# Hybrid decoder layer: value-pass sums taken from PSUM by DVE, the norm factor moved behind the value passes, and the sliding-window keys used as filler

## The chip, the cores and the metric

The kernel runs on one NeuronCore of a Trainium2 chip, as a single launch. The metric is the device time of one execution in microseconds, the median of several. The core has five engines that run side by side: PE (TensorE, matrix products and transposes), DVE (VectorE), ACT (ScalarE), POOL (GpSimd) and SP, whose queue issues nearly all DMA here. PE reads SBUF and writes PSUM, which the kernel divides into banks of 128 x 512 fp32: four called `z`, two `m`, two `o`.

## The reference

One decoder layer on 512 tokens of width 2048, in fp32, cut to what matters:

```python
h = rmsnorm(x, ln_mix)
proj = h @ w_in                        # 2048 x 4608
sb_q, sb_k, sb_v, sw_q, sw_k, sw_v = split(proj)   # 1024 1024 1024 | 1024 256 256
sb_o = stick_breaking_attention(sb_q, sb_k, sb_v)  # 16 heads of 64, causal
sw_o = sliding_window_sink_attention(sw_q, sw_k, sw_v, sinks, slopes)
                                       # 16 query heads, 4 key/value heads, window 128
mixed = concat(rmsnorm(sb_o, sb_out_norm), rmsnorm(sw_o, swa_out_norm))
x = x + mixed @ w_out
h = rmsnorm(x, ln_ffn)
x = x + (silu(gate) * up) @ w_down     # gate, up = h @ w_gate_up; width 5632
return rmsnorm(x, ln_final)
```

## The kernel before

**Precision.** Each fp32 operand of a product is split into a high part (rounded, by ACT) and a low part (the difference, by DVE). A product is then three PE products: high by high, high by low, low by high. The splits of weights are called `whi` and `wlo` (`split`, lines 220 and 221), those of the normalized input `hhi` and `hlo` (`split_scaled`, lines 272 and 273). PE therefore computes only at the pace at which ACT and DVE split.

**The queue of slabs.** Most projections are a list `queue` of weight slabs of 512 KB, each with its groups of three products. `step()` emits one group; at the third group of a slab it loads the two slabs behind it and splits the next. `pull(ns)` emits groups worth `ns` of the planner's time (648 ns for a feature group), `drain(mark)` all up to a mark, `defer(n, fn)` calls `fn` after `n` groups. So slabs are *filler*: they are pulled between the steps of the attention loops. The framework may reorder instructions of an engine against program order by its own cost estimate, except those called through `pV`, `pA`, `pG`, `pT` and every `dma`, which keep their order on their engine.

**First phase, while x arrives.** `add_kq` (line 534) puts eight slabs of 256 rows into the queue. Each has 512 columns: the 256 sliding-window key columns and the first 256 query columns, loaded by two DMAs (slab 0 by four). `prep(s)` first calls `h_make(kt)` for the row tiles that the slab needs: PE transposes four 128 x 128 blocks of x into a PSUM bank, `split_scaled` makes `hhi` and `hlo` with the gain, and POOL adds the two into `hf`. The norm factor of a row is not needed for this; it is a scale on tokens, applied at evacuation. `x_squares` sums the squares. `rstd1_make` (line 343) makes the factor from them, on DVE and ACT, four groups after slab 5; `rstd1_rows` broadcasts it along rows, by four products of `ones` with a scaled identity `dg` (`row_bc`, line 290).

**Value passes.** The stick-breaking value projection is done in seven products instead of eight (a Strassen-like scheme, `ValuePass`, line 568) for each of two halves `g` of the rows: 28 slots, each with one product of 12 PE instructions. Its weight-side sums are POOL's (`sum`: differences of loaded blocks). Its activation-side sums are formed from `hf` by POOL as well, in blocks of 128 x 1024 (`diff`, `s1`, `s2`, `s4`), and each is split by ACT (`form(p, "h")`) and DVE (`form(p, "l")`) into a tile `vf`. What happens in which slot is written out by hand in a table (`at_slot`), with the stages load, sum, late and take. The stage load issues on SP. Behind the slots the value tiles are scaled with the norm factor and split into `vst` (`value_split`).

**Stick-breaking loop.** 64 jobs (16 heads by four blocks of keys), whose filler is the eight query/key units `add_qk` of four slabs and the sliding-window value slabs of `add_swv`, up to `sb_mark`; the last value slab stays for the next loop. Each job pulls a fixed amount:

```python
SBFILL = SB_SLABS * 8 * 648.0 / 62     # SB_SLABS = 30; SBFILL per step of 66
```

**Sliding-window loop.** 16 jobs (four groups of four query heads, four token blocks). Its keys must be stacked into `kst` and its queries into `qst` (high and low parts one over the other, `stack_two` and `stack_one`, lines 685 to 699, on ACT and DVE). Keys and query group 0 come from `kq`, the tile that the first phase filled; groups 1 to 3 are projected by `add_swq` as filler inside this loop, and the output projection's first half (`add_outA`, 16 slabs) is filler behind them. The loop is preceded by `pull(16000.0)` and pulls 5200 per step. `kq` and the sliding-window value tile `swv` share one buffer.

**Behind it** come the second half of the output projection, the gated feed-forward part, also in passes of seven products, and the last norm. The change does not touch them.

Of the kernel before, what the change touches and what calls it, by code (L numbers as in the profile page):

```python
# [37 lines left out]
def tile_hymba(ctx: ExitStack, tc: tile.TileContext, x, ln_mix, w_in, sb_norm, swa_norm,  # L38
# [236 lines left out]
    def rstd_from(ss, n, scale, name):  # L275
# [292 lines left out]
    class ValuePass(Block):  # L568
# [37 lines left out]
        def block(self, q):  # L606
            x = hf[2 * self.g + int(q[1]) - 1]
            return x[:, :, 0:256] if q[0] == "1" else x[:, :, 256:512]

        def diff(self):  # L610
            self.s3 = self.tile("t", [P, 4, 256], bufs=3)
            pG.tensor_tensor(out=self.s3, in0=self.block("11"), in1=self.block("21"), op=ALU.subtract)

        def s1(self):
            pG.tensor_tensor(out=self.block("21"), in0=self.block("21"), in1=self.block("22"), op=ALU.add)

        def s2(self):
            pG.tensor_tensor(out=self.block("11"), in0=self.block("21"), in1=self.block("11"), op=ALU.subtract)

        def s4(self):  # L620
            pG.tensor_tensor(out=self.block("12"), in0=self.block("12"), in1=self.block("11"), op=ALU.subtract)
# [10 lines left out]
    vp = [ValuePass(g) for g in range(2)]
    for g in range(2):
        b0, u = 14 * g, vp[g]
        for k, q, i in ((-6, "12", 0), (-6, "22", 0), (-5, "11", 0), (-4, "12", 1), (-3, "22", 1), (-2, "11", 1),
                        (0, "21", 0), (1, "21", 1)):
# [1 line left out]
        for k, p, i in ((-3, "7", 0), (-2, "5", 0), (-1, "7", 1), (0, "5", 1), (1, "6", 0), (2, "6", 1),
                        (3, "4", 0), (4, "4", 1)):
            at_slot(b0 + k, "sum", u.sum, p, i)  # L640
        for k, fn, *args in ((-5, u.diff), (-5, u.s1), (-4, u.s2), (-4, u.form, "7", "h"), (-3, u.form, "7", "l"),
                             (0, u.form, "6", "h"), (1, u.form, "6", "l"), (4, u.form, "5", "h"), (5, u.form, "5", "l"),
                             (5, u.s4), (7, u.form, "3", "h"), (8, u.form, "3", "l")):
            at_slot(b0 + k, "late", fn, *args)
# [1181 lines left out]
```

## Time and profile before

| | us |
|---|---|
| median of 3 runs | 2033.25 (2032.68 to 2034.13) |
| the profiled execution's own time | 2032.92 |
| its span, first to last instruction | 2031.2 |
| PE busy | 2004.4 (99%) |
| DVE busy | 1505.8 (74%) |
| ACT busy | 1502.5 (74%) |
| POOL busy | 1123.3 (55%) |

The span is that of the engines' instructions; the execution's own time holds 1.7 us around it. Busy time is summed over an engine's instructions. A row of a timeline gives start, duration, engine, line, operation, output and inputs, count, and in brackets the idle time of that engine just before, with the instruction that ended it. Helpers record their callers' operations on their own line (most pinned calls are on L118), so rows are told apart by tile names. The granted clock is 1.00 when PE runs at full speed, 0.50 at half.

### The profile page before, as it was taken

Reading aid. Unit: us, or ns where it says so; the run is one execution under the profiler, and the core shown is the slowest. Engines: PE = TensorE matmul, PEld = TensorE weight load, DVE = VectorE, ACT = ScalarE, POOL = GpSimd, SP = SyncE. Lnnn points to the kernel's source line nnn. Section 1 sums busy time; section 2 is a strip of 40 time slices with the busy share of each in tenths; the row PEclk is TensorE's granted clock in tenths of the full one; section 3 lists DMA queues with packets and bytes.
Section 4 is the critical chain, followed back from the end, with each engine's and each line's share of the span. In section 5 each row is a group of like instructions: output and inputs, shape, how many; then the busy total and the mean of one; then the engine's idle time right before and its main releaser. Section 6 shows DMA issues by size and latency. Waiting matters only on the chain.

```text
span 2031.2 us, 29381 instructions
## 1 busy us (share of the span) xinstructions
PE 2004.4 (99%) x10364; PEld 1705.1 (84%) x10364; DVE 1505.8 (74%) x2016; ACT 1502.5 (74%) x2061; POOL 1123.3 (55%) x605
## 2 busy tenths in 40 slices
PE   9999999989999999999999999999999999999998
PEld 8778888878888888888888888888888888888886
DVE  5786888876984777777777777777777867767767
ACT  6675877755872468777777777777777788778787
POOL 5851444430000047666676666766667678878883
PEclk9999999989999999999999999999999999999999
DMA  7122222112234354535445354453444743433423
GB/s 240 66 78 83 63 63 71 58 39 84 73 120 134 120 163 123 136 102 137 117 117 140 101 134 123 111 140 105 129 129 106 270 161 104 169 142 104 171 89 115
DMA packets 286515, 240.24 MB, mean 118 GB/s; under 512 B 11168, under 2 KB 237536, under 8 KB 283936
## 3 DMA queue, kind: packets, MB, share of 16 engines
q1 hardware_dynamic: 285696, 235.71, 39.0%
q8 instruction: 82, 1.34, 0.3%
q0 software_dynamic: 288, 1.32, 0.2%
q10 hardware_dynamic: 384, 1.34, 0.2%
q14 instruction: 65, 0.53, 0.1%
HBM read 218.40 MB, written 19.92 MB: 117 GB/s over the span
## 4 chain that ended last, share of the span: by engine, by line
PE 74%; DVE 2%; ACT 1%; DMA 1%; issue 0%; DVEq 0%; POOL 0%; ACTq 0%; POOLq 0%
PE o L118 34%; PE m L118 28%; PE m L364 1%; PE m L366 1%; PE m L365 1%; PE o L365 1%; PE o L366 1%; PE o L364 1%; PE z L118 1%; DMA raw<-in_w_out_dram 1%; PE m L398 1%; PE m L397 1%; PE m L396 1%; DVE wlo L221 0%; PE z L1092 0%; PE o L398 0%
## 5 line engine op out<-in xcount | busy, mean ns | idle before, releaser
L118 POOL TENSOR_TENSOR t<-raw,t 128x1024 f32<-128x1024 f32 x111 | 282.2, 2543 | 276.9 <-ACT hp L118 262.5
L118 DVE TENSOR_TENSOR wlo<-t,hp 128x1024 fp32r<-128x1024 f32 x247 | 300.9, 1218 | 180.2 <-PE o L118 108.5
L118 ACT ACTIVATE whi<-t 128x1024 fp32r<-128x1024 f32 x247 | 262.1, 1061 | 127.6 <-PE o L118 76.9
L118 POOL TENSOR_TENSOR t<-raw,raw 128x1024 f32<-128x1024 f32 x114 | 296.9, 2607 | 26.8 <-issue 11.7
L118 PE MATMUL o<-hca,whi 128*128 128x512 f32 x880 | 307.5, 391 | 0.0
L118 DVE TENSOR_TENSOR wlo<-raw,hp 128x1024 fp32r<-128x1024 f32 x187 | 228.1, 1220 | 86.0 <-issue 52.1
L118 ACT ACTIVATE whi<-raw 128x1024 fp32r<-128x1024 f32 (+1 forms) x189 | 199.6, 1056 | 104.1 <-PE m L118 74.5
L118 ACT ACTIVATE hp<-t 128x1024 fp32r<-128x1024 f32 x247 | 249.1, 1008 | 0.7 <-POOL t L118 0.7
L118 PE MATMUL o<-hca,wlo 128*128 128x256 f32 x880 | 244.0, 280 | 0.0
L118 ACT ACTIVATE hp<-raw 128x1024 fp32r<-128x1024 f32 x191 | 192.7, 1009 | 3.3 <-DMA raw<-in_w_down_dram 2.3
L118 PEld LDWEIGHTS o<-hca,whi 128*128 128x128 f32 x880 | 164.2, 187 | 35.8
L118 PE MATMUL m<-hca,whi 128*128 128x512 f32 x528 | 186.3, 392 | 1.1 <-DVE hca L118 1.1
L221 DVE TENSOR_TENSOR wlo<-raw,whi 128x1024 fp32r<-128x1024 f32 x87 | 109.6, 1260 | 88.1 <-ACT whi L220 87.5
L220 ACT ACTIVATE whi<-raw 128x1024 fp32r<-128x1024 f32 x87 | 91.7, 1054 | 102.8 <-PE o L366 40.2
L118 PEld LDWEIGHTS o<-hca,wlo 128*128 128x128 f32 x880 | 165.6, 189 | 0.4
L118 PE MATMUL m<-whi,dca 128*128 128x512 f32 x592 | 146.9, 389 | 0.0
L118 PE MATMUL o<-whi,dca 128*128 128x512 f32 x592 | 146.8, 389 | 0.0
L118 PE MATMUL m<-hca,wlo 128*128 128x256 f32 x528 | 146.3, 280 | 0.0
L118 PEld LDWEIGHTS o<-whi,dca 128*128 128x128 f32 x592 | 111.1, 188 | 23.0
L118 PEld LDWEIGHTS m<-whi,dca 128*128 128x128 f32 x592 | 111.0, 188 | 23.1
L396 PE MATMUL m<-hhi,whi 128*128 128x512 f32 x320 | 130.3, 407 | 0.0
L118 PE MATMUL m<-hcs,whi 128*128 128x512 f32 x352 | 125.9, 392 | 0.0
(384 smaller groups left out, 5304.2 us busy)
## 6 DMA issues: line engine op xcount, KB each, us to landing
raw<-in_w_gate_up_dram SPq DMA_DIRECT2D x348, 256.0 KB, 5.2
raw<-in_w_down_dram SPq DMA_DIRECT2D x68, 512.0 KB, 4.7
raw<-in_w_in_dram SPq DMA_DIRECT2D x78, 256.0 KB, 3.1
raw<-in_w_out_dram SPq DMA_DIRECT2D x32, 512.0 KB, 4.6
raw<-in_w_in_dram SPq DMA_DIRECT2D x28, 512.0 KB, 3.6
aT<-w SPq DMA_DIRECT2D x44, 256.0 KB, 3.4
xd<-aT SPq DMA_DIRECT2D x10, 1024.0 KB, 7.7
rx<-in_w_down_dram SPq DMA_DIRECT2D x20, 512.0 KB, 6.1
```

The lines of the kernel that those rows point to most:

```text
L118: return lambda *a, **k: tc.keep_in_program_order(fn(*a, **k))
L220: A.activation(out=hi, in_=raw, func=AF.Copy)
L221: V.tensor_tensor(out=lo, in0=raw, in1=f(hi), op=ALU.subtract)
L364: mm(o, lhsT=lh[:, sl], rhs=hi[:, j, :], start=first, stop=False, skip_group_check=halves)
L365: mm(o, lhsT=lh[:, sl], rhs=lo[:, j, :], start=False, stop=False, skip_group_check=halves)
L366: mm(o, lhsT=ll[:, sl], rhs=hi[:, j, :], start=False, stop=(k == nslab * a - 1), skip_group_check=halves)
L396: mm(o, lhsT=wh, rhs=xh, start=(k == 0), stop=False)
L397: mm(o, lhsT=wh, rhs=xl, start=False, stop=False)
L398: mm(o, lhsT=wl, rhs=xh, start=False, stop=(k == KT - 1))
```

## The change

1. **Sums from PSUM.** `hf` and POOL's four block sums go. `h_make` now hands the transposed bank to `left_sums(kt, pb)`. For the first four row tiles of a half, POOL adds 256 columns of high and low part, and DVE later subtracts that from the other 256 columns, read from PSUM and multiplied with the gain; for the next four tiles DVE does three such operations. They are kept in `vsum` and emitted behind the split of the row tile after. The four sums of a half live in two `v8` tiles (`vleft`).
2. **`form(p, "l")`** moves from DVE to POOL, and into the stage `sum`; loads and sums get other slots. The sum for product 4 is written over that for product 6.
3. **The norm factor** is made behind the last value slot, pinned in order on DVE and ACT (`pV`, `pA`); its broadcast goes by ACT and is deferred by ten groups.
4. **First phase: four query tiles** (512 adjacent columns, one DMA per slab, two for slab 0) instead of two key and two query tiles; two of the four evacuations by DVE.
5. **Keys as filler.** The key columns and query group 2 become eight slabs ahead of `add_swv`, evacuated into a new tile `kq2`. Query group 3 stays in the sliding-window loop. `pull(16000.0)` goes; the stacks of key pair 1 and query group 2 are made in steps 5 and 6 of the loop, in buffers that the input's splits have left.

```diff
@@ load
         if i == 0:
             for j in range(a):
-                for k, src in enumerate(srcs):
-                    dma(out=raw[:, j, k * n:(k + 1) * n], in_=src[j * P:(j + 1) * P, :])
+                dma(out=raw[:, j, :], in_=srcs[0][j * P:(j + 1) * P, :])
@@ h_make
-            hf.append(v8.tile([P, 4, 512], F32, tag="v8", name="hf"))
-        pG.tensor_tensor(out=hf[kt // 4][:, kt % 4, :], in0=f(h_hi[kt]), in1=f(h_lo[kt]), op=ALU.add)
+        if kt > 1:
+            while vsum:
+                vsum.pop(0)()
+        left_sums(kt, pb)
+
+    def left_sums(kt, pb):
+        g, j, gc = kt // 8, kt % 4, gcol[:, kt:kt + 1]
+        if kt % 8 == 0:
+            vs = [v8.tile([P, 4, 512], F32, tag="v8", name="vs") for _ in range(2)]
+            for k, p in enumerate("5736"):
+                vleft[g, p] = vs[k // 2][:, :, (k % 2) * 256:(k % 2) * 256 + 256]
+        s1, s3, s4, s2 = (vleft[g, p][:, j, :] for p in "5736")
+        a, b = pb[:, 0:256], pb[:, 256:512]
+
+        def stt(out, x, y, op):
+            V.scalar_tensor_tensor(out=out, in0=x, scalar=gc, in1=y, op0=ALU.mult, op1=op)
+
+        if kt % 8 < 4:
+            pG.tensor_tensor(out=s1, in0=f(h_hi[kt])[:, 256:512], in1=f(h_lo[kt])[:, 256:512], op=ALU.add)
+            vsum.append(lambda: stt(s3, a, s1, ALU.subtract))
+        else:
+            vsum.append(lambda: (stt(s1, b, s1, ALU.add), stt(s2, b, s3, ALU.subtract), stt(s4, a, s2, ALU.subtract)))
@@ rstd1_make, rstd1_rows
-        V.tensor_reduce(out=sst, in_=ss1, axis=AX.X, op=ALU.add)
-        rs1["c"] = rstd_from(sst, NT, 1.0 / D, "rstd1")
+        pV.tensor_reduce(out=sst, in_=ss1, axis=AX.X, op=ALU.add)
+        rs1["c"] = rstd_from(sst, NT, 1.0 / D, "rstd1", pV, pA)
...
-        rs1["b"] = row_bc(rs1["c"], "rbc1")
+        rs1["b"] = row_bc(rs1["c"], "rbc1", pz())
@@ add_kq
-                    A.activation(out=kq[0][:, c, :], in_=o, func=AF.Copy)
+                    if c % 2:
+                        A.activation(out=kq[0][:, c, :], in_=o, func=AF.Copy)
+                    else:
+                        V.tensor_copy(out=kq[0][:, c, :], in_=o)
...
-            queue.append(dict(srcs=[win[rows, C_SWK:C_SWK + 256], win[rows, C_SWQ:C_SWQ + 256]], a=2, b=512, big=None,
+            queue.append(dict(srcs=[win[rows, C_SWQ:C_SWQ + 512]], a=2, b=512, big=None,
@@ ValuePass.form and its table
-                pV.tensor_tensor(out=hl[:, :, 256:512], in0=src, in1=f(hl)[:, :, 0:256], op=ALU.subtract)
+                pG.tensor_tensor(out=hl[:, :, 256:512], in0=src, in1=f(hl)[:, :, 0:256], op=ALU.subtract)
...
-        for k, q, i in ((-6, "12", 0), (-6, "22", 0), (-5, "11", 0), (-4, "12", 1), (-3, "22", 1), (-2, "11", 1),
+        for k, q, i in ((-6, "22", 0), (-6, "12", 0), (-5, "11", 0), (-4, "11", 1), (-3, "12", 1), (-2, "22", 1),
                         (0, "21", 0), (1, "21", 1)):
...
+        for k, fn, *args in ((-4, u.sum, "7", 0), (-3, u.sum, "5", 0), (-2, u.form, "7", "l"), (-1, u.sum, "6", 0),
+                             (0, u.sum, "7", 1), (1, u.sum, "5", 1), (2, u.form, "6", "l"), (3, u.sum, "6", 1),
+                             (4, u.sum, "4", 0), (5, u.sum, "4", 1), (6, u.form, "5", "l"), (8, u.form, "3", "l")):
+            at_slot(b0 + k, "sum", fn, *args)
+        for k, p in ((-4, "7"), (0, "6"), (4, "5"), (7, "3")):
+            at_slot(b0 + k, "late", u.form, p, "h")
@@ behind the first phase, and behind the value slots
     drain_to(5, 3)
+    while vsum:
+        vsum.pop(0)()
     x_squares(4)
-    defer(4, rstd1_make)
...
     run(28, "take")
+    rstd1_make()
     open_z("psw")
...
-    defer(3, rstd1_rows)
-    defer(8, lambda: [value_split(1, t) for t in (3, 2, 1, 0)])
-    defer(14, kq_scale)
+    defer(10, rstd1_rows)
+    defer(12, lambda: [value_split(1, t) for t in (3, 2, 1, 0)])
+    defer(20, kq_scale)
...
+    kq2 = kqs.enter_context(tc.tile_pool(name="kq2", bufs=1, side="right", reuse_waits="tile")).tile([P, 4, 512], F32, name="kq2")
+    add_feat(win, [(C_SWK, 256)], two_m, lambda c, pb: k_evac(pb, kq2[:, c, :]))
+    add_feat(win, [(C_SWQ + 512, 256)], two_m, lambda c, pb: q_evac(pb, kq2[:, 2 + c, :]))
     add_swv()
@@ sliding window
-    for g in range(1, 4):
-        add_swq(g)
+    kst[0], qst[0], qst[1] = (v8.tile([P, 4, 512], F32R, tag="v8", name=n) for n in ("kst", "qst", "qst"))
+    stack_keys(0)
+    stack_queries(0, kq[0][:, 0:2, :])
...
+        def tiles():
+            kst[1], qst[2], qst[3] = act8("kst"), act8("qst"), act8("qst")
...
+    add_swq3()
+    swq3_end = len(queue)
...
-    pull(16000.0)
     at(swa_scores, 0)
+    stack_queries(1, kq[0][:, 2:4, :])
     for j in range(NJ + 2):
...
-        if j + 1 < NJ and jobs[j + 1][1] == 0:
-            drain(smarks[jobs[j + 1][0]])
+        if j == 5:
+            drain(swq3_end - 2)
+            stack_keys(1)
+        if j == 6:
+            stack_queries(2, kq2[:, 2:4, :])
+        if j == 10:
+            drain(swq3_end)
```

More of the change, by code (lines that the diff above doesn't have):

```diff
@@ L273, in split_scaled, with rstd_from @@
         V.scalar_tensor_tensor(out=lo, in0=ps_ap, scalar=g_ap, in1=f(hi), op0=ALU.mult, op1=ALU.subtract)
-    def rstd_from(ss, n, scale, name):
+    def rstd_from(ss, n, scale, name, V=V, A=A):
         v = sm.tile([P, n], F32, tag="rv", name="rv")
@@ L308, in tile_hymba @@
     h8 = [None, None]
-    h8s, hf = [], []
+    h8s, vsum, vleft = [], [], {}
     XC = [(0, 256), (256, 256), (512, 512), (1024, 512), (1536, 512)]
@@ L595, in sum @@
         def sum(self, p, i):
-            self.difference(p, i, self.raw["12", i] if p == "5" else self.tile("t", [P, 2, 512], bufs=3))
+            self.difference(p, i, self.raw["12", i] if p == "5" else self.t["6", i] if p == "4" else
+                            self.tile("t", [P, 2, 512], bufs=3))
         def left(self, p, k, half, c):
@@ L604, in left @@
             return vfm[self.g, p][:, k, c:c + P]
[L606 to L621, printed above, removed]
         def form(self, p, part):
-            src = self.s3 if p == "7" else self.block({"6": "11", "5": "21", "3": "12"}[p])
+            src = vleft[self.g, p]
             if part == "h":
@@ L634, in tile_hymba @@
         b0, u = 14 * g, vp[g]
-        for k, q, i in ((-6, "12", 0), (-6, "22", 0), (-5, "11", 0), (-4, "12", 1), (-3, "22", 1), (-2, "11", 1),
+        for k, q, i in ((-6, "22", 0), (-6, "12", 0), (-5, "11", 0), (-4, "11", 1), (-3, "12", 1), (-2, "22", 1),
                         (0, "21", 0), (1, "21", 1)):
             at_slot(b0 + k, "load", u.load, q, i)
[L638 to L644, printed above, removed]
+        for k, fn, *args in ((-4, u.sum, "7", 0), (-3, u.sum, "5", 0), (-2, u.form, "7", "l"), (-1, u.sum, "6", 0),
[4 more added lines that the diff above has]
+            at_slot(b0 + k, "late", u.form, p, "h")
         for k, p in enumerate(PD):
@@ L792, in kq_scale @@
         for c in range(4):
-            (k_evac if c < 2 else q_evac)(kq[0][:, c, :], kq[0][:, c, :])
-    defer(3, rstd1_rows)
-    defer(8, lambda: [value_split(1, t) for t in (3, 2, 1, 0)])
-    defer(14, kq_scale)
+            q_evac(kq[0][:, c, :], kq[0][:, c, :])
+    defer(10, rstd1_rows)
+    defer(12, lambda: [value_split(1, t) for t in (3, 2, 1, 0)])
+    defer(20, kq_scale)
     open_phase("sbp", 1)
@@ L973, in tile_hymba, with stack_keys, stack_queries, add_swq3 @@
     qst = [None] * 4
-    smarks = [0] * 4
-    def add_swq(g):
+    def stack_keys(c):
+        for e in range(2):
+            stack_two(kq2[:, c, :], e * HD, kst[c][:, 2 * e, :], kst[c][:, 2 * e + 1, :])
+    def stack_queries(g, src):
+        for c in range(2):
+            for e in range(2):
+                stack_one(src[:, c, :], e * HD, qst[g][:, c * 2 + e, :])
+    kst[0], qst[0], qst[1] = (v8.tile([P, 4, 512], F32R, tag="v8", name=n) for n in ("kst", "qst", "qst"))
+    stack_keys(0)
+    stack_queries(0, kq[0][:, 0:2, :])
+    def add_swq3():
         def done(c, pb):
-            if c == 0:
-                qst[g] = v8.tile([P, 4, 512], F32R, tag="v8", name="qst")
             qf = tmp(name="qf")
@@ L981, in done @@
             for e in range(2):
-                stack_one(qf, e * HD, qst[g][:, c * 2 + e, :])
-        add_feat(win, [(C_SWQ + g * 256, 256)], (lambda: [po(), po()]) if g == 1 else two_m, done)
-        smarks[g] = len(queue)
-    qst[0] = v8.tile([P, 4, 512], F32R, tag="v8", name="qst")
-    for c in range(2):
-        kst[c] = v8.tile([P, 4, 512], F32R, tag="v8", name="kst")
-        for e in range(2):
-            stack_two(kq[0][:, c, :], e * HD, kst[c][:, 2 * e, :], kst[c][:, 2 * e + 1, :])
-            stack_one(kq[0][:, 2 + c, :], e * HD, qst[0][:, c * 2 + e, :])
-    for g in range(1, 4):
-        add_swq(g)
+                stack_one(qf, e * HD, qst[3][:, c * 2 + e, :])
+        def tiles():
+            kst[1], qst[2], qst[3] = act8("kst"), act8("qst"), act8("qst")
+        n = len(queue)
+        add_feat(win, [(C_SWQ + 768, 256)], lambda: [po(), po()], done)
+        queue[n + 1]["post"] = tiles
+    add_swq3()
+    swq3_end = len(queue)
     mixA = [None] * 10
@@ L1134, in tile_hymba @@
         pull(SWFILL / 4)
+    kqs.close()
     drain()
```

1 line of the change is left out of this document (added).

## The prediction

> **What bounds the kernel now.** First I read the page: engines' busy shares and the TensorE clock.
>
> ```profile
> span 2031.2 us, 29381 instructions
> PE 2004.4 (99%) x10364; PEld 1705.1 (84%) x10364; DVE 1505.8 (74%) x2016; ACT 1502.5 (74%) x2061; POOL 1123.3 (55%) x605
> ...
> PEclk9999999989999999999999999999999999999999
> ```
>
> TensorE is the bound, and the change removes none of its products: the four query/key tiles of the first phase are 64 groups of three matmuls before and after, the other six tiles 96 groups, only in another order. So the time can move by PE's idle time, the clock lost behind it, and new waits, nothing else. Next, the busy time by stage, with my cuts at the places where PE is not full (columns: busy of PE, PEld, DVE, ACT, POOL, then clock, DMA share, GB/s):
>
> ```profile
> core 0: us, PE busy (x) PEld busy (x) DVE busy (x) ACT busy (x) POOL busy (x), PEclk, DMA share, GB/s
> 8.01:53.60 45.59, 45.49 (x226) 37.62 (x227) 27.11 (x34) 29.55 (x67) 27.56 (x22) 1.00 0.75 245
> 53.60:58.53 4.93, 0.39 (x3) 0.00 (x1) 4.93 (x4) 0.00 (x0) 4.85 (x3) 0.88 0.01 2
> 58.53:64.23 5.70, 5.70 (x14) 4.45 (x15) 4.38 (x2) 1.63 (x3) 5.62 (x3) 0.50 0.00 0
> 66.00:139.00 73.00, 72.87 (x321) 60.01 (x321) 56.31 (x59) 59.59 (x63) 52.50 (x21) 1.00 0.20 66
> 139.00:150.00 11.00, 8.90 (x41) 6.67 (x40) 10.22 (x16) 7.46 (x10) 1.07 (x4) 1.00 0.52 150
> 415.00:433.00 18.00, 14.26 (x78) 10.33 (x76) 16.33 (x31) 14.99 (x33) 8.75 (x15) 1.00 0.00 1
> 433.00:446.50 13.50, 10.60 (x39) 8.73 (x40) 9.70 (x22) 3.19 (x8) 2.47 (x4) 0.50 0.01 1
> 467.00:620.00 153.00, 151.76 (x767) 125.80 (x766) 132.59 (x324) 113.84 (x282) 8.81 (x7) 1.00 0.31 102
> ```
>
> Three seams lose time. **Seam 1**, 53.6 to 64.2: a stall of 4.54 us, and behind it 5.70 us at clock 0.50, of which half (2.85) is lost: 7.4. **Seam 2**, 139 to 150: 11.00 - 8.90 = 2.1. **Seam 3**, 415 to 446.5: 18.00 - 14.26 = 3.7 idle, then 13.50 - 10.60 = 2.9 idle and half of 10.60 (5.3) lost to the clock: 11.9. Together 21.4 us. The x phase (8 to 53.6), the value passes (66 to 139) and the sliding-window stage (467 to 620) are full. What makes each seam, from the timelines and the waits of PE:
>
> ```profile
> 53.60 0.39 PE L544 MATMUL m<-hlo,whi 128*128 128x512 f32 x1
> 58.53 0.79 PE L545 MATMUL m<-hhi,wlo 128*128 128x512 f32 x1 [4.54 <-DVE wlo L221]
> ...
> 48.08 1.04 ACT L220 ACTIVATE whi<-raw 128x1024 fp32r<-128x1024 f32 x1
> 48.21 1.83 DVE L283 TENSOR_TENSOR rt<-rr 128x4 f32<-128x4 f32 x1 [0.51 <-ACT rr L281]
> 50.27 2.26 DVE L285 TENSOR_SCALAR rt<-rt 128x4 f32<-128x4 f32 x1
> 52.76 4.58 DVE L298 TENSOR_SCALAR dg<-ident,rstd 128x128 f32<-128x128 f32 x2
> 57.26 1.21 DVE L221 TENSOR_TENSOR wlo<-raw,whi 128x1024 fp32r<-128x1024 f32 x1
> 148.23 0.47 DVE L298 TENSOR_SCALAR dg<-ident,rstd 128x128 f32<-128x128 f32 x2
> ...
> 50.10 4.86 POOL L118 TENSOR_TENSOR hf<-hf 128x1024 f32<-128x1024 f32 x2
> 57.33 3.36 POOL L118 TENSOR_TENSOR raw<-raw,rx 128x1024 f32<-128x1024 f32 x1
> ```
> ```profile
> PE o L118 <- ACT whi L118: 1.0, 1, 1.0
> PE z L299 <- DVE dg L298: 1.1, 1, 1.1
> ...
> PE z L1041 <- DVE qst L699: 1.8, 3, 0.9
> PE z L900 <- DVE e L862: 1.2, 1, 1.2
> PE m L364 <- DVE swv L273: 1.1, 1, 1.1
> ```
>
> Seam 1: the norm factor's small operations sit on DVE in front of the last weight split. Two 128x128 products that take 0.47 us together when POOL is idle took 4.58, and a 128x4 one 2.26, each ending as POOL's long sum ended. Seam 2: ACT's weight copy stood behind the first scaled value splits, and the factor's broadcast waited for DVE. Seam 3: the filler runs dry, and DVE has eight heads of key and query stacking to do among the last head's own steps.
>
> **The change part by part.**
>
> *Norm factor behind the value passes.* The chain leaves DVE's queue at 47 to 57 us. ACT's half of the last split ended at 49.1, so it can run about 50, ahead of PE's need at 53.6. Seam 1's 7.4 goes, if what takes DVE's place is cheap:
>
> ```profile
> L273 DVE SCALAR_TENSOR_TENSOR hlo<-z,gcol,hhi 128x512 fp32r<-128x512 f32 x16 | 11.2, 744 | 4.9 <-ACT hhi L272 4.9
> L298 DVE TENSOR_SCALAR dg<-ident,rstd 128x128 f32<-128x128 f32 x2 | 4.6, 2329 | 0.0
> ...
> L273 DVE SCALAR_TENSOR_TENSOR swv<-m,rstd,swv 128x256 fp32r<-128x256 f32 x3 | 1.4, 480 | 2.5 <-ACT swv L272 2.5
> ...
> L118 POOL TENSOR_TENSOR hf<-hhi,hlo 128x512 f32<-128x512 f32 x16 | 21.1, 1342 | 23.5 <-DVE hlo L273 23.5
> L118 POOL TENSOR_TENSOR t<-raw,raw 128x1024 f32<-128x1024 f32 x8 | 21.9, 2746 | 9.6 <-DMA raw<-in_w_in_dram 7.4 <-ACT whi L118 2.2
> ```
>
> *Sums by DVE from PSUM.* One sum for each of 8 row tiles and three for each of the other 8: 32 operations of 256 columns. The nearest row is the 256-wide one with a PSUM input, 0.48 us: 15.4 us more on DVE from 8 to 54. DVE had 27.1 busy there, 5.6 of it the norm chain: 27.1 - 5.6 + 15.4 = 36.9 of 45.6 us, 81%. Does that delay a split that PE needs? The tightest place is a block of two row tiles with three sums between them:
>
> ```profile
> 22.62 1.03 PE L118 MATMUL z<-ident,xt 128*128 128x128 f32 x8
> 28.95 1.47 PE L118 MATMUL z<-ident,xt 128*128 128x128 f32 x12
> ...
> 24.71 1.40 DVE L273 SCALAR_TENSOR_TENSOR hlo<-z,gcol,hhi 128x512 fp32r<-128x512 f32 x2
> ```
>
> Transposes at 22.6, splits at 24.7 to 26.1; with three sums between, the second ends at 27.5. Its products come one group of eight behind the slab's start (27.6), at about 30.3: 2.8 us of slack. The sums run one row tile late, so they do not wait for POOL's add, and the bank is reused four tiles on. Cost 0, covered by that slack. POOL does 8 adds of half the size (estimate from 1.34: 0.67 each, 5.4 us for 21.1) and loses the eight block sums; it gets eight low-part subtractions from DVE at 2.4 to 2.75. In the value passes it keeps its count, one operation per slot or less.
>
> *Loads.* Slabs with 512 adjacent columns save nine of SP's issues; PE is packed behind 8 us, so 0. The value passes' loads are reordered; the last lands in time:
>
> ```profile
> 47.31 0.88 SPq L100 DMA_DIRECT2D raw<-in_w_in_dram  x2
> ...
> DMA to landing us min/median/max: 4.5/5.2/6.1
> ...
> 460.14 1.23 DVE L221 TENSOR_TENSOR wlo<-raw,whi 128x1024 fp32r<-128x1024 f32 x1 [4.21 <-ACT whi L220]
> 465.58 1.23 DVE L221 TENSOR_TENSOR wlo<-raw,whi 128x1024 fp32r<-128x1024 f32 x1 [4.21 <-ACT whi L220]
> ```
>
> A filler slab is 5.44 us (460.14 to 465.58), a slot of the value passes half of it, 2.72. Last landing: 48.2 + 5.2 = 53.4. The passes now begin near 59; the sum on that load (product 3) is needed at 59 + 3 x 2.72 - 2.2 = 65 (two copies of 1.1 stand between). Four POOL operations of 2.4 to 2.75 from 53.4 on end by 64; the product that needs the fourth begins at 72.6, so it is needed at 70. Bounds of what the passes lose: 0 (they lose 0.13 now) to 8 (rival C); I take 0.5, since the margins are a few us.
>
> *Seam 2.* The value splits can no longer get ahead of the weight copy, and the broadcast, on ACT, is deferred by ten groups (6.8 us); its first reader comes after four slabs (21.8). Gain 2.1. New: the factor's chain, pinned behind the last take, could hold ACT's copy for the second slab; bounds 0 to 2, the size of the seam itself. I take 1.0.
>
> *Keys and queries as filler.* By the planner's costs the sticks' loop pulls 66/62 x 30 x 5.18 + 4.0 = 169.5, and has 28 slabs of 5.18 and three of 5.18 (value): 160.7. It runs dry 8.8 before its end, as seam 3 shows. Eight slabs more (43.5 us measured) leave some 33 behind the loop, in which the last head and the first stacks (half as many) hide. Seam 3's 11.9 goes. (The late value columns are still evacuated into the buffer that the stacked tiles hold, seam 3's wait of 1.1; it now comes free after four more stacks, some 2.8 us of DVE, while PE goes on in the other pair of banks: 0, and 1.1 if it does not.) Two of the first phase's four evacuations move to DVE, 0.7 each: the bank's next product comes two tiles later, 0. In exchange the sliding-window loop starts without the 16 us pull in front and has 21 slabs (114 us) for 18 steps. PE's own work there: 151.8 less about 20 slabs (109) is 43; so it has 43 + 114 = 157 us against a loop of about 150, near balance, with DVE at 132.59/153 = 87%. DVE's change inside: two evacuations and a group's stack fewer, one key stack more, about even. Bounds for the loop: -1.2 (today's idle) to +6 (half of seam 3 again); I take +2.0.
>
> **Sum**: 2032.9 (the profiled execution: 2031.2 of span, 1.7 around it; the median is 2033.25) - 7.4 + 0.5 - 2.1 + 1.0 - 11.9 + 2.0 = **2015.0**.
>
> **The rivals.**
>
> B. The attention seam moves instead of going: the first sliding-window jobs have no filler in front, the scores wait for the stacks, and half of 11.9 returns. For it: DVE is the engine PE waits for in that seam, and 87% leaves little. Against: 33 us of dense filler now stand between. 2015 + 6 = 2021.
>
> C. POOL and DVE shut each other out in the value passes. DVE has 28 splits of 1.22 (34.2 us), POOL 27 operations of 2.4 (64.8), of which some 14 us run before the first product; if two-input operations of the two exclude each other, 50.8 + 34.2 = 85.0 against 28 x 2.72 = 76.2: +9, so 2024. Against: from 66 to 139 POOL was busy 52.5 and DVE 56.3 of 73.0, with PE full. The Trainium skill, "SBUF — State Buffer", section "SBUF: two separate sides", states that rule: the shared port pair is an exclusive lock, taken also by a DVE operation with two SBUF inputs against a GpSimd one that reads SBUF. By it the change, which moves subtractions to POOL, would end at C's time. The trace bears out the stretched 128x128 products, not a full exclusion of two-input operations.
>
> D. Both come true, and the change does not do what it says: 2015 + 6 + 9 = 2030.
>
> E, slower. DVE becomes the bound while x arrives: the sums stand in order in front of the row tiles' low parts. Place: the seven slabs from 15 to 54 us. Each stall like seam 1's costs 7.4 with its clock, and the change gains 17.9: two such stalls leave it near today's time (2030), from the third on it is slower: 2037, and with four 2045. For it: 81% of an in-order queue. Against: 2.8 us of slack where three sums stand together, and it would take sums of over 1 us.
>
> **How the numbers follow.** The likeliest, all three seams closed, 0.60: 2015, by its bounds 2010.5 (no new loss at all, and 1.2 of the loop's idle gone) to 2020. B 0.15, C 0.11, D 0.08, E 0.06. A change of 0.2% (4 us) is about what a measurement of this kernel can tell from none. Faster is the first three, 0.86; same D, 0.08; slower E, 0.06. The range takes in B and C: 2010 to 2026, which leaves out 0.14 and the tails.
>
> **What would show it.** Right: PE without a gap from 8 to the passes' end near 136, clock 1.00 there; the passes' first product near 59; the factor's chain on DVE near 137 with operations of 0.2; no clock of 0.50 around the end of the sticks; stacks beside filler. Wrong: PE waits for a row tile's low part before 54 (E); waits for a weight copy behind a POOL sum in the passes (C); waits on scores, transposes or DVE's softmax steps at 440 to 590 (B), or filler exhausted before the loop's last job.

## The result, and the profile after

The changed kernel takes **2010.26 us** (median of 4 runs, 2009.47 to 2010.75) against 2033.02 (2032.68 to 2034.13, 4 runs): a ratio of 0.9887, 95% interval 0.987 to 0.9904, so some 23 us faster. The forecast was 2015.0, between 2010 and 2026, so the result lies 4.8 below the forecast and at the lower edge of the range: two of the four runs (2009.47 and 2009.9) are below it. The profiled execution of after took 2010.75, with a span of 2009.0. All times and ranges here are of fast runs; one run of the filler experiment (2465 us, granted clock 0.752) and two of before measured beside the experiments (3873 and 6546 us) were slow ones and are not counted.

The page of after, the lines that answer to those of before:

```profile
span 2009.0 us, 29374 instructions
...
PE 1992.6 (99%) x10364; PEld 1700.1 (85%) x10364; DVE 1498.7 (75%) x2038; ACT 1503.0 (75%) x2063; POOL 1106.1 (55%) x597
...
PEclk9999999999999999999999999999999999999999
```

PE does the same 10364 products. The 8 in the clock's row is gone. The busy time by stage, cut at the same places of the program (columns as before):

```profile
7.69:51.50 43.81, 43.07 (x216) 35.66 (x217) 35.48 (x60) 29.38 (x65) 14.21 (x14) 1.00 0.71 239
51.50:56.40 4.90, 4.90 (x23) 4.06 (x22) 1.15 (x2) 0.00 (x0) 4.90 (x3) 1.00 0.65 241
...
59.13:135.29 76.16, 76.16 (x337) 63.08 (x336) 49.79 (x54) 60.74 (x63) 51.98 (x22) 1.00 0.22 70
135.29:146.00 10.71, 10.71 (x51) 8.60 (x50) 8.57 (x17) 7.53 (x16) 1.07 (x4) 1.00 0.35 101
...
415.00:434.00 19.00, 18.26 (x85) 14.59 (x85) 17.65 (x29) 14.07 (x24) 5.86 (x8) 1.00 0.18 56
434.00:447.00 13.00, 13.00 (x81) 11.71 (x81) 6.25 (x7) 2.65 (x3) 1.29 (x1) 1.00 0.41 122
447.00:460.00 13.00, 13.00 (x111) 13.00 (x110) 2.86 (x4) 2.12 (x2) 0.34 (x1) 1.00 0.26 82
460.00:510.00 50.00, 49.96 (x282) 43.15 (x282) 46.82 (x124) 40.38 (x104) 0.81 (x2) 1.00 0.26 85
510.00:532.00 22.00, 19.17 (x95) 15.30 (x95) 20.65 (x55) 18.20 (x44) 2.26 (x1) 0.92 0.31 96
```

The three seams are closed: PE is full, at clock 1.00, where 51.50, 135.29 and 434.00 begin. One new hole stands at 510 to 532, at clock 0.92, with DVE busy 20.65 of 22.00. The longest waits of PE in the whole trace show it too:

```profile
PE m L384 <- DVE wlo L220: 1.9, 1, 1.9
PE o L118 <- POOL ones L127: 1.2, 1, 1.2
PE m L118 <- DVE hca L118: 1.1, 1, 1.1
PE m L564 <- DVE wlo L220: 0.7, 1, 0.7
```

The 0.7 is a new wait for a weight's low part at 15.5 us; the 1.2 stands at the very start, ahead of PE's first instruction, and the 1.1 in a later stage (at 733 us). Both were there before, and the change leaves them alone.

Where the time came from is read by the lead of after at the same instruction, the start in before less that in after:

| the first | before | after | lead |
|---|---|---|---|
| product | 8.01 | 7.69 | 0.32 |
| value product | 66.28 | 59.13 | 7.15 |
| stick query/key product | 144.22 | 135.29 | 8.93 |
| stick score | 173.18 | 163.22 | 9.96 |
| product of the output's second half | 643.54 | 621.30 | 22.24 |

The lead stays at 9.95 through the sticks' loop, to about 390. So the first phase gave 7.1 (0.3 of it ahead of the first product, so 6.8 for seam 1, net of the new wait of 0.7), the value passes with seam 2 gave 2.8, seam 3 with the sliding-window loop 12.3.

For seam 3 and the loop I count PE's loss from the starts of its products: the time from one start to the next, less the median of that distance for the shape, summed in bins of 10 us. This sees the half clock and idle time alike, and holds within about 0.5 us. The seam, 410 to 450, lost 16.9 in before and loses 1.2 in after; the sliding-window loop, from 500 on, lost 3.7 and loses 5.5. By the lead the loop lost 3.4 more than before, as the remainder (-15.7 + 3.4 = -12.3); what the count from 500 on does not hold of it lies in bits below 1 us from 460 on.

### The profile page after: what moved, and what is told of

Same layout as the page of the kernel before. It is cut to its first block, busy times and chain, and to the rows that moved or that the text cites. A ratio compares the mean times of both kernels' runs of the same rounds, so it can differ in the third digit from the quotient of the medians.

```text
span 2009.0 us, 29374 instructions
## 1 busy us (share of the span) xinstructions
PE 1992.6 (99%) x10364; PEld 1700.1 (85%) x10364; DVE 1498.7 (75%) x2038; ACT 1503.0 (75%) x2063; POOL 1106.1 (55%) x597
## 4 chain that ended last, share of the span: by engine, by line
PE 96%; DVE 2%; ACT 1%; issue 0%; DMA 0%; SPq 0%; POOL 0%; DVEq 0%; ACTq 0%
PE o L118 36%; PE m L118 30%; PE m L415 4%; PE m L416 4%; PE m L417 4%; PE m L384 2%; PE m L385 2%; PE m L383 2%; PE z L118 1%; PE o L385 1%; PE o L384 1%; PE o L383 1%; PE o L935 1%; PE z L851 1%; PE z L850 1%; PE z L914 0%
## 5 line engine op out<-in xcount | busy, mean ns | idle before, releaser
L118 DVE TENSOR_TENSOR wlo<-t,hp 128x1024 fp32r<-128x1024 f32 x247 | 301.1, 1219 | 184.3 <-PE o L118 113.0
L118 POOL TENSOR_TENSOR t<-raw,t 128x1024 f32<-128x1024 f32 x111 | 281.9, 2539 | 281.9 <-ACT hp L118 269.5
L118 ACT ACTIVATE whi<-t 128x1024 fp32r<-128x1024 f32 x247 | 262.0, 1061 | 125.8 <-PE o L118 76.0
L118 PE MATMUL o<-hca,whi 128*128 128x512 f32 x880 | 307.5, 391 | 0.0
L118 POOL TENSOR_TENSOR t<-raw,raw 128x1024 f32<-128x1024 f32 x114 | 294.5, 2586 | 21.3 <-issue 10.8
L118 DVE TENSOR_TENSOR wlo<-raw,hp 128x1024 fp32r<-128x1024 f32 x187 | 228.3, 1221 | 92.2 <-issue 52.1
L118 ACT ACTIVATE whi<-raw 128x1024 fp32r<-128x1024 f32 (+1 forms) x189 | 199.8, 1057 | 105.4 <-PE m L118 75.2
L118 ACT ACTIVATE hp<-t 128x1024 fp32r<-128x1024 f32 x247 | 249.1, 1009 | 2.5 <-POOL t L118 2.5
L118 PE MATMUL o<-hca,wlo 128*128 128x256 f32 x880 | 244.0, 280 | 0.0
L118 ACT ACTIVATE hp<-raw 128x1024 fp32r<-128x1024 f32 x191 | 192.8, 1009 | 3.8 <-DVE wlo L118 2.2
L118 PEld LDWEIGHTS o<-hca,whi 128*128 128x128 f32 x880 | 164.2, 187 | 35.8
L118 PE MATMUL m<-hca,whi 128*128 128x512 f32 x528 | 186.3, 392 | 1.1 <-DVE hca L118 1.1
L118 PEld LDWEIGHTS o<-hca,wlo 128*128 128x128 f32 x880 | 165.6, 189 | 0.4
L118 PE MATMUL m<-whi,dca 128*128 128x512 f32 x592 | 146.9, 389 | 0.0
L118 PE MATMUL o<-whi,dca 128*128 128x512 f32 x592 | 146.9, 389 | 0.0
L118 PE MATMUL m<-hca,wlo 128*128 128x256 f32 x528 | 146.3, 280 | 0.0
L118 PEld LDWEIGHTS m<-whi,dca 128*128 128x128 f32 x592 | 111.1, 188 | 23.0
L118 PEld LDWEIGHTS o<-whi,dca 128*128 128x128 f32 x592 | 111.1, 188 | 23.1
L118 PE MATMUL m<-hcs,whi 128*128 128x512 f32 x352 | 125.9, 392 | 0.0
```

Source lines behind the costliest of these rows:

```text
L118: return lambda *a, **k: tc.keep_in_program_order(fn(*a, **k))
```

## The experiments

**The three parts by themselves.** First the norm factor, put back into DVE's queue four groups after slab 5 in the kernel after:

```
     x_squares(4)
+    defer(4, rstd1_make)
...
     run(28, "take")
-    rstd1_make()
```

> The changed kernel with the norm factor made where it was before, on DVE four groups behind slab 5, and its broadcast by DVE; all else as changed. Theory (each seam has its own cause, and the factor's small operations on DVE are that of the first two): the stall at about 51 to 56 us comes back with its half clock, and the value splits get ahead of the weight copies again: 7 to 10 us on 2010.3, so 2017 to 2020. Rival (the sums taken from PSUM freed POOL, and without POOL's long sums the chain on DVE is cheap): 2010 to 2013.

Measured: 2017.39 us (2016.15 to 2018.43), 7.1 more than after, in the theory's range. Its timeline, rows of DVE and POOL alone:

```profile
50.57 1.22 DVE L220 TENSOR_TENSOR wlo<-raw,whi 128x1024 fp32r<-128x1024 f32 x1
51.93 2.40 POOL L118 TENSOR_TENSOR vf<-vs,vf 128x1024 fp32r<-128x1024 f32 x1 [2.32 <-ACT vf L118]
51.98 2.37 DVE L282 TENSOR_TENSOR rt<-rr 128x4 f32<-128x4 f32 x1 [0.19 <-ACT rr L280]
54.28 4.75 POOL L118 TENSOR_TENSOR t<-raw,raw 128x1024 f32<-128x1024 f32 x2
54.38 2.31 DVE L283 TENSOR_TENSOR rt<-rt,rv 128x4 f32<-128x4 f32 x1
56.72 2.34 DVE L284 TENSOR_SCALAR rt<-rt 128x4 f32<-128x4 f32 x1
...
59.29 2.46 DVE L297 TENSOR_SCALAR dg<-ident,rstd 128x128 f32<-128x128 f32 x2
61.68 0.68 DVE L571 COPY kq<-m 128x512 f32<-128x512 f32 x1
```

The last weight split is now ahead of the chain and on time, so the stall stands elsewhere than forecast: four operations of the chain end with a POOL sum (those that meet none keep 0.16), and the `kq` evacuation behind them frees PE's bank 3.0 us late (`L118 <- DVE kq`), with the half clock after it. By the starts of the same products, this run is behind after by 3.4 at the first value product, 6.2 at the first stick query/key product and 7.2 at the first stick score, so the 7.1 holds seam 2 as well as seam 1. The price is that of the chain beside POOL's sums, wherever PE meets DVE's queue next.

Then the factor's place alone, in the kernel before (the same lines, the other way round):

> The kernel before with one part of the change: the norm factor made behind the value passes, pinned, its broadcast by ACT and deferred by ten groups. Theory: seams 1 and 2 go, seam 3 stays: 2033.0 - 7.4 - 2.8 = 2022.8, between 2021.5 and 2024.5. Rival (POOL's sums are what delays DVE there): half of it or less, 2028 to 2033.

Measured: 2025.57 (2025.2 to 2027.47), 7.7 less than before (2033.28 on that chip), short of the 10.2 forecast and outside its range of 2021.5 to 2024.5. Seams 1 and 2 are gone, and a wait that neither kernel has stands in the value passes (PE's longest wait of the first 160 us, then rows of the timeline):

```profile
PE m L118 <- ACT whi L118: 1.9, 1, 1.9
```
```profile
50.54 1.06 ACT L118 ACTIVATE vf<-t 128x1024 fp32r<-128x1024 f32 x1 [1.10 <-POOL t L118]
50.58 6.61 POOL L118 TENSOR_TENSOR hf<-hf 128x1024 f32<-128x1024 f32 x2
...
57.15 2.40 POOL L118 TENSOR_TENSOR t<-raw,raw 128x1024 f32<-128x1024 f32 x1
...
70.14 1.03 ACT L118 ACTIVATE hp<-t 128x1024 fp32r<-128x1024 f32 x1 [3.69 <-POOL t L118]
```

With the seam closed, the passes begin 7 us earlier, and POOL, which works without a break from 48.1 to 72.4 with two block sums (6.61) in that stretch, makes its weight sums late. The passes take 78.6 from their first product to the next stage's, 76.2 in after; these 2.4 are nearly all that the gain fell short by (2.5), and show what taking the sums off POOL is good for beside the first part. The whole change leads before by 9.96 at the first stick score, this part alone by 7.4.

The sums by DVE from PSUM alone, in the kernel before (`left_sums`, the low parts on POOL, the new table of slots; the factor early):

> The kernel before with one part of the change: activation sums by DVE from PSUM, low parts of the forms by POOL, the new slots of loads and sums; norm factor early, key tiles first. Theory: the first stall stays, since the factor's chain is still in DVE's queue beside POOL's weight sums: 2031 to 2035. Rival (less POOL work lets the chain through): 2024 to 2028.

Measured: 2030.06 (2028.7 to 2031.94), ratio 0.9986 (0.9976 to 0.9996), 3.2 less. That lies between the theory (2031 to 2035) and the rival (2024 to 2028), so neither forecast holds. The chain is again drawn out (2.37, 2.31, 2.34 and 2.51), but the last weight split stands ahead of it, as in the first run: seam 1's wait of 4.5 is gone, and PE waits 1.4 (at 16.5 us) and 1.6 (at 63.7) for low parts of weights and 0.8 and 1.1 in seam 2.

Queries first and keys as filler alone, in the kernel before:

> The kernel before with one part of the change: four query tiles in the first phase, keys and query group 2 as eight slabs of filler ahead of the value slabs, no pull in front of the sliding-window loop. Theory: seams 1 and 2 stay, seam 3 goes and the loop loses some 5 us: 2033.0 - 12.3 = 2020.7, between 2019 and 2023. Rival (the seam only moves into the loop): 2026 to 2033.

Measured: 2019.79 (2019.12 to 2019.83), ratio 0.9932 (0.9913 to 0.9952), 13.5 less: as expected. Seam 1's wait of 4.6 stays; PE's busy time in 400 to 450 is 49.26 of 50.00; and the loop has the hole of after already:

```profile
PE m L544 <- DVE wlo L220: 4.6, 1, 4.6
PE m L364 <- DVE wlo L220: 1.9, 1, 1.9
```

Together -7.7 - 3.2 - 13.5 = -24.4, against -22.8 for the whole: the parts overlap by under 2 us. The overlap lies ahead of the sticks: at the first stick score the three lead before by 7.4, 4.9 and 1.2, 13.5 in sum, and the whole change by 9.96, for the factor and the sums both relieve seam 1. From there on the third part gives 12.2 alone and 12.3 in the whole.

**What closed seam 3: more filler, or fewer stacks?** Two runs in the kernel before, with less filler asked for in each step of the sticks' loop, meant to leave some for its end and behind it:

```
-SB_SLABS = 30
+SB_SLABS = 28      (the second run: 24)
```

> The kernel before, with the sticks' loop planned for 28 slabs of filler in place of 30, so that by the planner's costs it pulls 158.6 of the 160.7 us that it has and does not run dry. Before is 2033.3. Theory 'filler' (seam 3 is PE without filler, all of it): the loop keeps its filler to the end and the seam's 16.8 us, as counted from the starts of PE's products, go: 2015 to 2020. Theory 'both' (1.84 + 3.69 = 5.5 us between 410 and 430 are the missing filler, the 11.2 us between 430 and 450 are DVE's eight heads of key and query stacking, which PE waits for with no filler behind the loop): 2026 to 2030, with the wait for qst and the half clock near 433 to 446 still there. Theory 'stacks alone': 2032 to 2034.

> The kernel before, with the sticks' loop planned for 24 slabs of filler in place of 30 (28 changed nothing): the loop takes some 26 of its 31 slabs, and what is left, about 25 us, is drained between the loop and the sliding-window scores, with the eight heads of stacking on DVE as before. Before is 2033.2. Theory 'filler behind the loop' (seam 3's 16.8 us are the tail of the last head and the stacks with no product of PE's beside them, so filler there closes it, whatever the number of stacks): 2017 to 2023, with PE over 95% from 420 to 450; the swv wait of 1.1 may stay. Rival 'half the stacks' (eight heads on DVE are too long for the seam even beside filler, and the change closed it by having four): 2026 to 2032, waits for qst still there. A third: a loop with a sixth less filler waits for its own DVE and ACT chains, and gives back what the seam gains: 2028 to 2036, with the lost time before 410.

Measured: 2035.48 with 28 (2034.87 to 2036.59) and 2037.68 with 24 (2036.48 to 2038.65); before is 2033.2. Both are slower than before and outside every range forecast for them. With 28, the seam (400 to 450) loses 16.9, as before. With 24, it still loses 15.5, and the sticks' loop (200 to 410) 10.4 in place of 2.7. Stages of the second run, PE's waits from 400 on, and its last filler product ahead of the scores with the next one:

```profile
430.00:440.00 10.00, 7.43 (x35) 5.21 (x34) 9.69 (x17) 8.25 (x15) 3.94 (x5) 0.81 0.01 2
440.00:450.00 10.00, 7.64 (x25) 5.48 (x26) 6.65 (x16) 2.28 (x6) 1.79 (x2) 0.50 0.01 2
```
```profile
PE z L903 <- DVE l L868: 2.5, 3, 1.0
PE z L1041 <- DVE qst L699: 1.5, 3, 0.8
```
```profile
434.47 0.28 PE L366 MATMUL m<-whi,hlo 128*128 128x256 f32 x1
435.19 0.39 PE L1041 MATMUL z<-kst,qst 128*128 128x256 f32 x1 [0.44 <-DVE qst L699]
...
449.82 0.58 PE L364 MATMUL m<-whi,hhi 128*128 128x256 f32 x1
```

The edit did not do what it was meant to. For 15.3 us, in which the last head's products wait for their low parts (`l`) and the scores for the stacks, PE has no filler product; in before it is 15.7. The reason stands in the program: `sb_begin` drains the queue up to a head pair's own query/key slabs before that pair starts, so what a step does not pull is pulled there in a lump. By the planner's costs these drains take 7.8 us with 30 slabs, 16.8 with 28 and 34.4 with 24, and the queue is empty at the 60th or 61st of the 66 steps in all three. So neither run had filler behind the loop, and neither tests the theory "filler behind the loop" or its rival "half the stacks". The time lost before 410, which the third theory forecast, is seen; the lumps are the likely cause, but that is not shown.

The reverse, in the kernel after: the stacks as there, and the filler used up.

```
-SB_SLABS = 30
+SB_SLABS = 37.5
```

> The kernel after, with the sticks' loop planned for 37.5 slabs of filler in place of 30: by the planner's costs it asks for 210.9 of the 202.1 us that it has, and so runs dry 8.8 before its end, as the kernel before does; the four heads of stacking at the seam stay as in after. After is 2010.3, and its seam loses 1.2 us of PE where that of before loses 16.8. Theory 'both needed' (24 slabs in the kernel before showed that filler does not close the seam beside eight heads of stacks; here four heads without filler): half of the loss returns, 8 us, and the wait with the half clock: 2016 to 2021. Rival 'half the stacks is all': the seam stays closed or loses 1 to 4: 2008 to 2014. A third, 'filler is all': the whole seam returns, 14 to 17 us: 2023 to 2028.

Measured: 2019.97 (2019.55 to 2020.78), 9.7 more than after, in the range of "both needed". The seam, now at 450 to 480 since the loop holds more filler, loses 10.3 in place of 1.2:

```profile
460.00:480.00 20.00, 13.83 (x77) 12.15 (x77) 17.66 (x44) 9.98 (x28) 2.86 (x4) 0.83 0.11 28
```
```profile
468.73 0.69 DVE L704 TENSOR_TENSOR qst<-kq,qst 64x512 fp32r<-64x512 f32 x1
...
469.45 0.84 ACT L271 ACTIVATE swv<-m,rstd 128x256 fp32r<-128x256 f32 x2 [2.39 <-DVE qst L704]
...
470.18 1.05 ACT L219 ACTIVATE whi<-raw 128x1024 fp32r<-128x1024 f32 x1
...
471.29 0.79 PE L415 MATMUL o<-hhi,whi 128*128 128x512 f32 x1 [4.76 <-ACT whi L219]
```

Its form is worth a look: PE waits 4.76 for a weight copy, which stands on ACT behind the evacuation of `swv`, which waited for the last query stack (the two share a buffer). So that buffer, priced at 0 to 1.1 in the prediction, takes part in a wait of this size once no filler covers it.

Here the edit did what it says, and it isolates the filler: the stacks are those of after. Over the runs, the seam's loss goes with the time that PE is without a filler product:

| run | no filler product on PE | loss of the seam | operations for stacks on DVE there |
|---|---|---|---|
| before | 15.7 (427.5 to 443.3) | 16.9 | 16 |
| before, 28 slabs | 15.4 (430.6 to 446.0) | 16.9 | 16 |
| before, 24 slabs | 15.3 (434.5 to 449.8) | 15.5 | 16 |
| after, filler used up | 9.4 (461.9 to 471.3) | 10.3 | 14 |
| after | 2.0 (458.4 to 460.4) | 1.2 | 14 |

The stacks differ less than "eight heads against four": 16 operations of DVE in before (11.0 us), 14 in after (8.7), of which 10 stand ahead of the first scores in the program. In after the last one ends at 436.2, 23 us before the first score:

```profile
435.55 0.69 DVE L704 TENSOR_TENSOR qst<-kq,qst 64x512 fp32r<-64x512 f32 x1
```
```profile
459.38 0.36 PE L1061 MATMUL z<-kst,qst 128*128 128x256 f32 x1
```

So filler is needed: shown. Whether fewer stacks are needed as well is open: no run has the stacks of before beside filler, and the 23 us of room speak against it.

**The new hole in the loop.** DVE's part of it in after, a query stack in the middle of the steps and the weight split that PE waits for:

```profile
515.26 0.69 DVE L704 TENSOR_TENSOR qst<-kq,qst 64x512 fp32r<-64x512 f32 x1
...
516.85 2.09 DVE L704 TENSOR_TENSOR qst<-kq,qst 64x512 fp32r<-64x512 f32 x3
...
525.84 1.22 DVE L220 TENSOR_TENSOR wlo<-raw,whi 128x1024 fp32r<-128x1024 f32 x1
...
527.12 0.65 PE L384 MATMUL m<-wlo,mhi 128*128 128x512 f32 x1 [1.85 <-DVE wlo L220]
```

Four ways to relieve it, each an edit of after. The two stacks spread over four steps:

```
-        if j == 5:
+        if j == 4:
             drain(swq3_end - 2)
-            stack_keys(1)
-        if j == 6:
-            stack_queries(2, kq2[:, 2:4, :])
+        if j in (4, 5):
+            stack_keys(1, (j - 4,))
+        if j in (6, 7):
+            stack_queries(2, kq2[:, 2:4, :], (j - 6,))
```

> The kernel after, with the second key stack and the third query stack of the sliding-window loop, which stand in steps 5 and 6, spread over steps 4 to 7, half a stack in each (drain of their filler one step earlier). After is 2010.3. Theory 'burst' (the wait of 1.9 us for a weight split at 527 and the half clock behind it come from these two stacks in DVE's queue, 98% full from 510 to 532): about 4 of the loop's 5 us of loss go, 2005.5 to 2008.5, no clock of 0.50 near 530. Rival 'balance' (DVE is simply full in this stretch, and what is moved shows up a step later): 2009.5 to 2011.5, with a wait of the same size elsewhere between 500 and 540. A third: draining a step earlier takes filler from the steps ahead: 2011.5 to 2014.

The same stacks' DVE part on POOL (`stack_keys(1, G)`, `stack_queries(2, ..., G)`):

> The kernel after, with the subtractions and copies of the same two stacks (second keys, third queries, steps 5 and 6) on POOL, which is nearly idle there, and ACT's part as it is. After is 2010.3. Theory 'DVE's queue': 12 operations of 0.4 to 0.7 us, some 7 us, leave DVE between 500 and 527, the weight split is on time: 2005.5 to 2008.5, no clock of 0.50 near 530. Rival 'ACT or balance': the split's other half by ACT is late as well, or the stretch is full otherwise: 2009.5 to 2011.5. A third: POOL's operations take twice as long and shut out DVE's two-input ones, so the scores that need the stacks wait: 2011 to 2014.

More filler for each step (`SWFILL = 5900.0` for 5200.0):

> The kernel after, with 5.9 planner-us of filler for each step of the sliding-window loop in place of 5.2 (18 steps: 12.6 us more, out of the some 17 us that PE still does from this queue behind the last step). After is 2010.3. Theory 'balance' (from 500 to 532 DVE is full; more PE work for each step gives DVE time, so PE waits less): of the loop's 7 to 8 us of loss 2 to 4 go, 2006.5 to 2008.5. Rival 'chain' (the waits are of the steps' own softmax chain and the order of DVE's queue, and more filler also brings more weight splits to DVE): 2009.5 to 2011.5. A third: the queue is empty before the last step, and the end of the loop has a seam of its own: 2011.5 to 2015.

Half the maxima:

```
-        for b in range(2):
-            V.tensor_reduce(out=mx[:, 2 * b:2 * b + 2], in_=B.s[b][:, :, 0:kw], axis=AX.X, op=ALU.max)
+        V.tensor_reduce(out=mx[:, 0:2], in_=B.s[0][:, :, 0:kw], axis=AX.X, op=ALU.max)
+        V.tensor_copy(out=mx[:, 2:4], in_=mx[:, 0:2])
```

> The kernel after, with the row maximum of the sliding-window scores taken over the first pair of heads alone and copied for the second (left out: 16 of 32 reductions, 15 us of them 0.68 each with the copy at 0.16, so DVE is relieved of some 8 us in the loop, 0.5 in each step, and the softmax chain is 0.5 shorter). After is 2010.3. Theory 'DVE's queue sets the loop's loss' (stack bursts spread, put on POOL, and more filler moved the loss of 7 to 8 us without removing it, because DVE is 95 to 98% full from 480 to 532): 3 to 5 of it go, 2005 to 2007.5. Rival 'ACT and the order of the steps': DVE falls below 93% from 480 to 532 and the waits stay, for ACT's or the filler's operations: 2009 to 2011.

| edit | us | loss 500 to 620 | longest wait there |
|---|---|---|---|
| after | 2010.26 | 5.5 | 1.9, weight split (DVE) |
| spread | 2010.47 (2010.18 to 2011.24) | 5.8 | 0.8, weight split (DVE) |
| on POOL | 2009.77 (2009.54 to 2011.05) | 4.3 | 0.8, scaled scores (ACT) |
| more filler | 2010.97 (2010.61 to 2011.64) | 5.6 | 1.5, weight split (DVE) |
| half the maxima | 2009.38 (2008.43 to 2009.54) | 3.9 | 0.7, weight split (DVE) |

The leading theory's range is missed in all four. The burst is not the cause: spread, it leaves the same loss in smaller waits, as its rival "balance" said. More filler per step does not help either, so that run's own theory falls; the losses of after, spread and more filler differ by less than the 0.5 that the count can tell. Work taken from DVE buys a little, 1.2 of loss on POOL and 1.6 with half the maxima, less than the 2 to 5 forecast. In that last run DVE is as full as before where the loss is, and ACT close behind:

```profile
510.00:520.00 10.00, 9.41 (x49) 7.55 (x48) 9.64 (x24) 9.55 (x24) 1.45 (x1) 1.00 0.40 119
520.00:532.00 12.00, 10.71 (x58) 8.44 (x57) 11.78 (x37) 9.95 (x23) 0.00 (x0) 1.00 0.23 77
```

So DVE's queue seems to set a part of the loss; whether ACT's order sets the rest was not tried. None of the four beats the changed kernel by more than its runs vary; the one lowest leaves out maxima.

**Low parts of the summed forms back on DVE**, in the kernel after (`pV` for `pG` in `form`):

> The kernel after, with the low parts of the four summed forms of each value pass back on DVE (eight subtractions of two SBUF inputs), as in the kernel before, and all else as after. After is 2010.3. Theory 'lock' (POOL and DVE shut each other out only where both DVE inputs are in SBUF; the weight splits of the passes have one input in PSUM): these eight take 1.3 to 3.4 us in place of 1.22 where they meet a POOL sum, the 28 weight splits stay at 1.22, PE stays full or loses up to 2 us: 2010 to 2013. Rival 'no lock' (all DVE operations keep their length): mean of the eight within 0.1 of 1.22, 2009.5 to 2010.8. Rival 'full exclusion of two-input operations': the weight splits beside POOL's sums are stretched too, 2013 to 2019.

Measured: 2011.14 (2009.84 to 2011.23), no change that can be told. DVE's groups of the stage:

```profile
L118 DVE TENSOR_TENSOR wlo<-raw,hp 128x1024 fp32r<-128x1024 f32 x12 | 14.6, 1217 | 5.5 <-issue 3.4 <-PE m L118 1.8 <-PE o L118 0.3
L118 DVE TENSOR_TENSOR vf<-vs,vf 128x1024 fp32r<-128x1024 f32 x8 | 12.6, 1579 | 1.7 <-ACT vf L118 1.7
```

The eight moved subtractions have a mean of 1.58: two that begin well inside a POOL operation take 3.42 and 1.89, the other six 1.22. The 28 weight splits stay at 1.22, also the 14 of them that begin while POOL works. The theory "lock" holds, and both rivals fall. In after it is POOL's operations that are drawn out instead (below).

## Why the prediction came out right, step by step

**Factor behind the passes**, -7.4 forecast for seam 1, where the lead gives 6.8, and -8.5 with seam 2 (-7.4 - 2.1 + 1.0), where the run that undoes it gives 7.1 and the run that does it alone 7.7. The mechanism was right, and the size within 1.5. The small operations of the chain, now behind the passes, take 0.17:

```profile
138.43 0.17 DVE L118 TENSOR_TENSOR rt<-rr 128x4 f32<-128x4 f32 x1 [0.51 <-ACT rr L118]
```

The estimate of DVE while x arrives held as well: 36.9 of 45.6 us forecast, 35.48 of 43.81 measured (81% both), and the sums take what their nearest row said:

```profile
L349 DVE SCALAR_TENSOR_TENSOR vs<-z,gcol,vs 128x256 f32<-128x256 f32 x32 | 13.9, 476 | 1.3 <-POOL vs L118 1.2
```

Cost 0 was nearly right; 0.7 of it came as the wait at 15.5. Rival E, DVE as the bound, did not come.

**Value passes +0.5, seam 2 -2.1 + 1.0**: -0.6 forecast, -2.8 measured. The two new losses were over-estimated by 1.5: PE is full for 76.16 of 76.16 in the passes and 10.71 of 10.71 behind them. The chain pinned behind the last take held up no weight copy. The passes also run 1.78 faster from first product to the next stage's, which holds the first of seam 2's waits, the 1.0 for a weight copy.

**Seam 3 -11.9, loop +2.0**: -9.9 forecast, -12.3 measured, of two errors of opposite sign. The seam was under-sized, 16.9 by the starts of the products: I took busy rows at full speed as work, but a product's row lasts 0.39 at full clock and 0.80 at half, while products in a row start 0.23 apart, so idle time hides in busy time where products stand alone. That term should have been -15.7. The loop's +2.0 was +3.4, with DVE full at 510 to 532 (20.65 of 22.00) rather than on a mean of 87%. The cause as I put it, the filler running dry, is borne out: used up again, it gives back 9.7. But the dry stretch was taken as 8.8 us, without the lumps that `sb_begin` drains (7.8); with them it is 16.6 by the planner's costs, and the trace shows 15.7. By the same count the eight slabs leave 24.6 behind the loop, not 33. That half as many stacks had a part in it is not shown.

The likeliest case, all three seams closed, came true. Its lower bound is 2010.3 by its own terms (the prediction gives 2010.5), and the result lies on it: the new losses in the passes and seam 2 did not come, and the seam's larger size outweighs the loop's. That 2010.26 is still inside the range is a matter of 0.3 us, less than the runs vary.

**Rival B** did not come as described: the first scores do not wait for stacks. The loop loses 1.8 more from 500 on, in a wait for a weight split, where B asked 6. **Rival D**, B and C together, falls with them.

**Rival C** did not come, and my reading of its rule was wrong. I counted the 28 weight splits as operations with two SBUF inputs and so called the trace's evidence "not a full exclusion". They subtract `hp`, which lies in PSUM (`zs[1].tile(..., tag="hp")`), so they are not of that kind: in after, 22 of the 28 begin while a POOL operation runs, and none takes over 1.22. Where both inputs are in SBUF, one waits for the other. Two pairs of POOL and DVE in after:

```profile
42.59 2.38 POOL L118 TENSOR_TENSOR t<-raw,raw 128x1024 f32<-128x1024 f32 x1 [2.93 <-DMA raw<-in_w_in_dram]
42.97 3.09 DVE L220 TENSOR_TENSOR wlo<-raw,whi 128x1024 fp32r<-128x1024 f32 x1 [0.17 <-ACT whi L219]
...
50.16 1.22 DVE L220 TENSOR_TENSOR wlo<-raw,whi 128x1024 fp32r<-128x1024 f32 x1
50.31 3.32 POOL L118 TENSOR_TENSOR vf<-vs,vf 128x1024 fp32r<-128x1024 f32 x1 [1.98 <-ACT vf L118]
```

Whichever begins first keeps its length (2.38, 1.22), and the other ends about its own length behind it: 42.97 + 3.09 = 46.06 is 1.09 behind 44.97; 50.31 + 3.32 = 53.63 is 2.25 behind 51.38. This agrees with the Trainium skill, "SBUF — State Buffer", section "SBUF: two separate sides", which calls the shared port pair an exclusive lock for DVE operations with two SBUF inputs against GpSimd ones that read SBUF. By that rule the change takes eight such operations out of DVE's queue in the passes, which spoke for it, not against.

## What to carry to other kernels

Price a seam by the starts of the products, not by busy time: the loss includes the half clock behind a stall and the length that lone products show. Before a move is charged with DVE and POOL shutting each other out, look where each operand lies: a subtraction with one input in PSUM is free of it, and a chain of 128x4 operations in SBUF is not. A seam in which the next loop waits for another engine's backlog closes when filler lasts over the backlog; here it came back when the filler was used up, with the backlog as small as in after. An edit that is meant to leave filler has to be seen in the trace, by the starts of the filler's products: a forced drain elsewhere can take it all the same.

## What the runs showed of the hardware that was not expected

Size does not shield an operation from POOL: three 128x4 operations of 0.16 to 0.17 us took 2.31 to 2.37 in a row in the run with the early factor, one POOL sum each. It includes a TENSOR_SCALAR with one tensor input (2.34), so two tensor inputs in SBUF are not the only case here. (The same section of the Trainium skill names DVE operations in a two-port mode as the other; no run here shows an operation's mode.) In the run with stacks on POOL the same is seen the other way: POOL's subtraction of 64x512 takes 1.33 there, DVE's 0.69, so moving it costs POOL twice the time and buys PE little.
